# Output projection pairs: the residual sum is turned at once, without a provisional per-token factor

## The chip, the cores and the metric

The kernel runs on one core of a Trainium2 chip. Its five engines work beside each other, each through its own queue in order: TensorE (PE, matrix products; its weight loads are listed as PEld), VectorE (DVE), ScalarE (ACT), GpSimd (POOL) and SyncE (SP, which here only issues the DMA transfers). The metric is device time in microseconds (us), and the median of the runs counts.

## The reference

One decoder layer on 512 tokens of width 2048, all in float32. The middle is mixed by two kinds of heads, which are not touched here. What matters is the passage from the heads to the feed-forward part:

```python
mix = jnp.concatenate([out_a.astype(x.dtype), out_b.astype(x.dtype)], axis=-1)
x = x + mix @ w_out[l]
h2 = rms_norm(x, norm2_g[l])
x = x + (jax.nn.silu(h2 @ w_gate[l]) * (h2 @ w_up[l])) @ w_down[l]
```

`rms_norm` multiplies each token's row by one over the root of its mean square (plus 1e-6), and each column by `norm2_g`. The factor of a token is one number per row, so it can be applied behind a product with `w_gate` or `w_up` as well as ahead of it. `w_gate` and `w_up` have 5632 columns.

## The kernel before, in words

**Products.** Every large product is done two blocks of 512 columns at a time (a "pair", class `Pair`), by a scheme with seven half-size products, P1, P5, P6, P3, P7, P2, P4 in this order, of sums of quarters of the weights and of the activations. Each of the seven runs over the depth in 4 steps (3 in one operand of the last projection). I call one product at one step a group. A group is 12 matmuls on PE: 8 with the rounded ("high") part of the weights, tile `wh`, and 4 with the remainder, tile `wl`. ACT makes `wh` (L332), DVE makes `wl` (L336) and, in four products of seven, the difference of two weight quarters ahead of that (L257). There are two buffers of each, so ACT and DVE run at most about two groups ahead of PE. A pair of 4 steps has 28 groups. The two output projection pairs are called A and B here (groups A0 to A27, B0 to B27). Behind them come 11 feed-forward pairs for `w_gate` and `w_up` (the first one's groups are F0, F1, ...), and 6 pairs for `w_down`.

**Operands.** The activations stand in memory with the depth on the partitions. `Operand` splits each of the seven sums of a step into a high and a low part (`split`: a cast on ACT, L176, a subtraction on DVE, L177), all 128x512. The operand of the feed-forward pairs, `opn`, is read back from the DRAM tiles `xn_d0` to `xn_d7`, each with two halves of 256 tokens: `operand_jobs` builds its steps 0 and 1 from `xn_d0` to `xn_d3` in full, and `early_job` and `late_jobs` build steps 2 and 3 from `xn_d4` to `xn_d7`, the early ones through a tile `top`.

**Closing a product.** Four of the products (P3, P7, P2, P4) end an output block of 256 tokens by 512 columns. `final_out` then adds the residual (`residual`: two loads into tiles `q` and `k`, two sums on DVE, L1251, or L1248 for the block behind P4), stores the sum to `x1_d`, and squares it on ACT with a row sum into `ss2` (L1275). Eight such blocks, four in each pair, make the whole new x. Each is turned for the feed-forward part by `transposed_store`: 8 PE transposes (L1073), 4 ACT copies out of PSUM that multiply by `norm2_g` (L1084, into tiles `oT` and `PT`), two stores to `xn_d`. I call this a turn, and number the turns 1 to 8.

**The provisional factor.** Ahead of a turn, `scaled_store` multiplies the two tiles by `prox`, on ACT (L1259, into `qT` and `kT`). `prox` is one over the root of the mean square of each token's first 1024 columns, made on POOL by a power (L160, L161) once pair A has closed its last block. So in pair B each closed block is scaled and then turned one group later, while the four blocks of pair A wait until pair A is over: `first_columns` reloads them from `x1_d` (L1304, tiles `T` and `v`), scales and turns them during B's first groups. Then `operand_jobs` builds steps 0 and 1. `output_scales` makes the factor `rs2`, that corrects the provisional one, from all of `ss2`, in two sums on DVE and five small POOL instructions; the feed-forward pairs apply it where they close (L283, L299, L1346).

**What sets the order.** `stream` writes out the groups of all pairs in one sequence. In each group, between the high and the low matmuls, it calls a step function. That runs what is due in a list `deferred` (filled by `later(n, f)`: n steps from now), and then one step of the first generator in `background`. What a step issues lands in the engines' queues at that place; the framework may then move it by a few instructions.

## Time and profile before

| | |
|---|---|
| median of 3 runs | 1976.02 us (1974.23 to 1976.25) |
| profiled execution, its own time | 1977.08 us |
| its span, first to last instruction | 1975.2 us |
| PE busy | 1930.5 us, 98% |
| DVE busy | 1653.7 us, 84% |
| ACT busy | 1096.0 us, 55% |
| POOL busy | 55.0 us, 3% |
| granted TensorE clock, mean | 0.996 |
| last group of pair A to the end of turn 8 | about 642 to 748 us from the start |

The profile lists, for each instruction, its start, its duration, its engine and line, and in brackets how long the engine sat idle ahead of it and what ended that. A row may merge several instructions of one kind (x8). Durations of neighbours on one engine can overlap a little, so the time that an instruction takes in a full queue is read from start to start.

### The profile page before, as it was taken

The numbers are of one execution on the slowest core, as the hardware profiler recorded it, in microseconds if no ns is written. First come the engines' busy times: TensorE is split into PE (matmuls) and PEld (weight loads), VectorE is DVE, ScalarE is ACT, GpSimd is POOL, SyncE is SP. The second block draws the span as 40 slices with busy tenths as digits, with TensorE's granted clock in tenths as the row PEclk, the third lists the DMA queues.
The fourth block names the chain that finished last, engine by engine and source line by source line (L and its number), as shares of the span: only waits on it lengthen the run. The fifth ranks groups of instructions, "written<-read, shape, count | busy, mean of one in ns | idle before, by whom it ended". The sixth has DMA issues, their size and how long they took to land.

```text
span 1975.2 us, 25806 instructions
## 1 busy us (share of the span) xinstructions
PE 1930.5 (98%) x9226; PEld 1669.3 (85%) x9226; DVE 1653.7 (84%) x1850; ACT 1096.0 (55%) x1600; POOL 55.0 (3%) x81
## 2 busy tenths in 40 slices
PE   7999999999999989999999999999999999999998
PEld 6888888887878777888888888888888888888887
DVE  7997777768789789878878878878879989989977
ACT  7664564566676666545545545545446646546443
POOL 0000130011000001000000000000000000000000
PEclk9999999999999999999999999999999999999999
DMA  7347354444666584443543443543445855855662
GB/s 277 125 166 266 116 189 162 143 159 160 202 215 231 194 275 159 177 168 129 177 166 133 174 166 127 176 165 129 176 165 167 292 206 183 293 190 177 235 213 75
DMA packets 184505, 360.45 MB, mean 182 GB/s; under 512 B 16198, under 2 KB 94863, under 8 KB 184376
## 3 DMA queue, kind: packets, MB, share of 16 engines
q1 hardware_dynamic: 184168, 358.72, 52.8%
q8 instruction: 72, 1.18, 0.2%
q14 instruction: 57, 0.47, 0.1%
q10 hardware_dynamic: 208, 0.08, 0.0%
...
## 4 chain that ended last, share of the span: by engine, by line
PE 79%; DVE 8%; DMA 8%; issue 3%; ACT 1%; SPq 1%; POOL 0%; DVEq 0%; ACTq 0%; POOLq 0%
PE acc L362 70%; DVE wl L336 3%; PE acc L430 3%; DVE wa L257 2%; PE bank L1073 1%; PE bank L980 1%; DMA k<-y_d 1%; PE bank L958 1%; DVE AS L177 1%; DMA T<-p_d 1%; DMA xn_d<-oT 1%; DMA k<-in_gw 1%; DVE seed L1251 1%; PE bank L973 0%; PE bank L430 0%
## 5 line engine op out<-in xcount | busy, mean ns | idle before, releaser
L362 PE MATMUL acc<-wh,AS 128*128 128x512 f32 x3008 | 713.5, 380 | 1.5 <-DVE AS L177 1.0
L362 PEld LDWEIGHTS acc<-wh,AS 128*128 128x128 f32 x3008 | 567.7, 189 | 84.0 <-DVE AS L177 1.8
L332 ACT CAST wh<-wa 128x1024 fp32r<-128x1024 f32 x376 | 394.0, 1048 | 400.3 <-PE acc L362 364.9
L362 PE MATMUL acc<-wh,AA 128*128 128x512 f32 x2256 | 536.4, 380 | 6.0 <-ACT wh L332 6.0
L336 DVE TENSOR_TENSOR wl<-wa,wh 128x1024 fp32r<-128x1024 f32 x376 | 457.0, 1219 | 80.1 <-ACT wh L332 47.5
L362 PEld LDWEIGHTS acc<-wh,AA 128*128 128x128 f32 x2256 | 426.5, 189 | 68.6 <-ACT wh L332 8.4
L362 PE MATMUL acc<-wl,AS 128*128 128x512 f32 x1504 | 394.4, 384 | 7.2 <-DVE wl L336 7.1
L362 PEld LDWEIGHTS acc<-wl,AS 128*128 128x128 f32 x1504 | 279.3, 189 | 59.3 <-DVE wl L336 19.0
L362 PE MATMUL acc<-wl,AA 128*128 128x512 f32 x1128 | 296.7, 385 | 0.4 <-DVE wl L336 0.4
L362 PEld LDWEIGHTS acc<-wl,AA 128*128 128x128 f32 x1128 | 210.6, 190 | 32.3 <-DVE wl L336 2.7
L332 ACT CAST wh<-wb 128x1024 fp32r<-128x1024 f32 x94 | 98.5, 1048 | 118.0 <-PE acc L362 114.7
L332 ACT CAST wh<-wc 128x1024 fp32r<-128x1024 f32 x94 | 98.4, 1046 | 111.2 <-PE acc L362 105.4
L332 ACT CAST wh<-wd 128x1024 fp32r<-128x1024 f32 x94 | 98.6, 1049 | 104.7 <-PE acc L362 99.8
L336 DVE TENSOR_TENSOR wl<-wc,wh 128x1024 fp32r<-128x1024 f32 x94 | 114.8, 1221 | 41.2 <-ACT wh L332 40.9
L336 DVE TENSOR_TENSOR wl<-wd,wh 128x1024 fp32r<-128x1024 f32 x94 | 114.6, 1221 | 39.1 <-ACT wh L332 30.2
L257 DVE TENSOR_TENSOR wa<-wc,wa 128x1024 f32<-128x1024 f32 x94 | 114.6, 1222 | 35.7 <-DMA wc<-in_w_gate 20.0
L336 DVE TENSOR_TENSOR wl<-wb,wh 128x1024 fp32r<-128x1024 f32 x94 | 114.4, 1218 | 7.0 <-ACT wh L332 6.6
L257 DVE TENSOR_TENSOR wb<-wd,wb 128x1024 f32<-128x1024 f32 x94 | 114.5, 1218 | 0.4
L257 DVE TENSOR_TENSOR wa<-wb,wa 128x1024 f32<-128x1024 f32 x94 | 113.6, 1219 | 0.8
L257 DVE TENSOR_TENSOR wa<-wd,wa 128x1024 f32<-128x1024 f32 x94 | 113.0, 1217 | 0.2
L299 DVE SCALAR_TENSOR_TENSOR seed<-acc,rs,seed 128x512 f32<-128x512 f32 x96 | 70.6, 746 | 29.6 <-PE acc L362 29.6
L283 ACT ACTIVATE seed<-acc,rs 128x512 f32<-128x512 f32 x96 | 60.8, 683 | 3.1 <-DMA wc<-in_w_in 1.7
...
## 6 DMA issues: line engine op xcount, KB each, us to landing
...
```

The source lines that it names most:

```text
L177: nc.vector.tensor_tensor(a[:, :, 1, :], src, a[:, :, 0, :].bitcast(F32), op=ALU.subtract)
L257: nc.vector.tensor_tensor(src, self.quarter(one, g), src, op=ALU.subtract)
L283: nc.scalar.activation(halves(t), unfolded(src[m]), AF.Copy, scale=self.scale(half, m))
L299: nc.vector.scalar_tensor_tensor(halves(seed[m]), unfolded(src[m]), self.scale(half, m), halves(seed[m]), op0=ALU.mult, op1=ALU.add,)
L332: nc.scalar.copy(high[k], sources[k])
L336: nc.vector.tensor_tensor(low[k], sources.pop(k), high[k].bitcast(F32), op=ALU.subtract)
L362: nc.tensor.matmul(p.dst[prod][m], a[:, jj, hl, m * P : (m + 1) * P], folded(w[:, jj, :]), start=fresh and g == 0 and len(terms) == 2 and ...
L430: recent["pe"] = nc.tensor.matmul(dst[prod][m], a[:, jj, hl, m * P : (m + 1) * P], folded(w[:, jj, :]), start=fresh and g == 0 and len(ter ...
L958: nc.tensor.matmul(lp[:, :n], qh[:, b * P : (b + 1) * P], kh[:, :n], start=True, stop=True)
L980: nc.tensor.matmul(op, vh[:, k, :], lgs[b][:, k * P : (k + 1) * P], start=(k == 0), stop=(k == b))
L1073: nc.tensor.transpose(bk[:, jj, m * P : (m + 1) * P], tiles[m][:, f : f + P], ident)
L1251: nc.vector.tensor_tensor(tiles[m], tiles[m], r, op=ALU.add)
```

## The change

Nothing is multiplied by a provisional factor any more. In both pairs, `final_out` gives the summed tiles themselves to `transposed_store`, one step after the sum, so turns 1 to 3 move from pair B into pair A, and turn 4 to B's second group. With that go the 8 reloads from `x1_d`, the 16 scalings L1259 and `prox`. `operand_jobs` is put into the background at turn 4, at B's second step instead of its first, but without the eight steps of `first_columns` ahead of it. The factor `rs2` is now that of the whole row, made in three parts, one step apart, in the feed-forward groups F1 to F3: a sum and a scaling on DVE; a logarithm and an exponential on ACT; a correcting step of three small DVE instructions. All POOL work on factors of this norm goes.

```diff
-    part2 = const([P, 4], "part2")
-    prox = const([P, 4], "prox")
+    ms2 = const([P, 4], "ms2")
+    rt2 = const([P, 4], "rt2")
...
-    def scaled_store(tiles, rows, half, dsts, k0):
-        xs = []
-        for m in range(2):
-            s = work(("qT", "kT")[m])
-            nc.scalar.activation(s, tiles[m], AF.Copy, scale=prox[:, rows[m] : rows[m] + 1])
-            xs.append(s)
-        return lambda: transposed_store(xs, half, dsts, g2[:, k0 : k0 + 4])
...
-            if second:
-                turn = scaled_store(tiles, rows, tok, xn_d[2 * ch : 2 * ch + 2], 4 * ch)
-
-                def rest():
-                    turn()
-                    if which == 1 and half == 1:
-                        background.extend(early_job(opn, g, tops[g], False) for g in (2, 3))
-                        background.append(late_jobs(opn, ((2, 3),), tops, bots, False))
-
-                later(1, rest)
-                if which == 0 and half == 1:
-                    output_scales()
-            elif which == 0 and half == 1:
-                nc.vector.tensor_tensor(part2, ss2[:, :, 0], ss2[:, :, 1], op=ALU.add)
-                rsqrt_mean(prox, part2, D // 2)
-                background.append(first_columns())
-                background.append(operand_jobs(opn, tops, bots, 0, 2))
+            dsts, gains = xn_d[2 * ch : 2 * ch + 2], g2[:, 4 * ch : 4 * ch + 4]
+
+            def turn():
+                transposed_store(tiles, tok, dsts, gains)
+                if not second and which == 0 and half == 1:
+                    background.append(operand_jobs(opn, tops, bots, 0, 2))
+                elif second and which == 1 and half == 1:
+                    background.extend(early_job(opn, g, tops[g], False) for g in (2, 3))
+                    background.append(late_jobs(opn, ((2, 3),), tops, bots, False))
+
+            later(1, turn)
+            if second and which == 0 and half == 1:
+                for n in range(3):
+                    later(1 + n, lambda n=n: output_scales(n))
...
-    def first_columns():
-        for ch in range(2):
-            for tok in range(2):
-                tiles = []
-                for m in range(2):
-                    r = work(("T", "v")[m])
-                    load(r, x1_d[2 * tok + m][:, 512 * ch : 512 * ch + 512])
-                    tiles.append(r)
...
-    def output_scales():
-        tmp2 = const([P, 4], "tmp2")
-        nc.vector.tensor_tensor(tmp2, ss2[:, :, 2], ss2[:, :, 3], op=ALU.add)
-        nc.vector.tensor_tensor(tmp2, tmp2, part2, op=ALU.add)
-        rsqrt_mean(rs2, tmp2, D)
-        nc.gpsimd.tensor_scalar(part2, part2, 2.0 / D, EPS, op0=ALU.mult, op1=ALU.add)
-        nc.gpsimd.tensor_tensor(part2, part2, phalf, op=ALU.pow)
-        nc.gpsimd.tensor_tensor(rs2, rs2, part2, op=ALU.mult)
+    def output_scales(part):
+        if part == 0:
+            nc.vector.tensor_reduce(ms2, ss2, axis=mybir.AxisListType.X, op=ALU.add)
+            nc.vector.tensor_scalar(ms2, ms2, 1.0 / D, EPS, op0=ALU.mult, op1=ALU.add)
+        elif part == 1:
+            nc.scalar.activation(rt2, ms2, AF.Ln)
+            nc.scalar.activation(rt2, rt2, AF.Exp, scale=-0.5)
+        else:
+            nc.vector.scalar_tensor_tensor(ms2, ms2, -0.5, rt2, op0=ALU.mult, op1=ALU.mult)
+            nc.vector.tensor_tensor(ms2, ms2, rt2, op=ALU.mult)
+            nc.vector.scalar_tensor_tensor(rs2, ms2, 1.5, rt2, op0=ALU.add, op1=ALU.mult)
```

The rows below are instructions in the order of one engine's queue. They carry buffer numbers, and line numbers of the kernel they come from: after the change L332 is L330, L1084 is L1082, L1275 is L1265, L176 is L174, L1088 is L1086, L1127 is L1125.

ACT at the start of pair B, before. The casts L332 are those of groups B2, B3 and B4:

```order
L332 CAST wh_1163_6000<-wa_1153_5961 128x1024
L1275 ACTIVATE L_1158_5983,ss2_209<-k_1156_5976 128x512
L332 CAST wh_1170_6036<-wa_1164_6002 128x1024
L1259 ACTIVATE qT_1161_5992<-T_1159_5988,prox_211 128x512
L332 CAST wh_1177_6063<-wa_1145_5923 128x1024
L1259 ACTIVATE kT_1162_5994<-v_1160_5990,prox_211 128x512
L1084 ACTIVATE oT_1167_6019<-bank_1166_6014,g2_91 128x256 x2
L1084 ACTIVATE PT_1169_6028<-bank_1168_6023,g2_91 128x256 x2
```

ACT at the same place, after. The casts L330 are those of B2, B3 and B4 again; `r` are tiles read back from `xn_d` for the operand:

```order
L330 CAST wh_1171_6041<-wa_1165_6013 128x1024
L174 CAST AA11_1179_6075<-r_1178_6073 128x2x256
L1265 ACTIVATE L_1169_6032,ss2_207<-q_1167_6025 128x512
L1265 ACTIVATE L_1170_6035,ss2_207<-k_1168_6028 128x512
L330 CAST wh_1180_6082<-wa_1172_6043 128x1024
L1082 ACTIVATE oT_1175_6060<-bank_1174_6055,g2_89 128x256 x2
L1082 ACTIVATE PT_1177_6069<-bank_1176_6064,g2_89 128x256 x2
L174 CAST AA22_1184_6099<-r_1183_6097 128x2x256
L330 CAST wh_1185_6106<-wa_1153_5957 128x1024
```

The scaling of the reloaded tile is gone from between the casts of B3 and B4. In its place the operand's first two casts, of tiles read back from `xn_d`, stand ahead of the casts of B3 and B4, and the copies there are those of turn 4.

SP around the end of pair A, after: its stores of turn 3 and what is queued behind them (before, `xn_d0` is first stored after the reloads from `x1_d`):

```order
L1244 DMA q_1167_6025<-in_x 128x512
L1244 DMA k_1168_6028<-in_x 128x512
L221 DMA wd_1208_6210<-in_w_out 128x1024
L221 DMA wd_1212_6232<-in_w_out 128x1024
L1086 DMA xn_d0_199<-oT_1156_5974 256x1x256
L1086 DMA xn_d1_200<-PT_1158_5983 256x1x256
L221 DMA wd_1218_6258<-in_w_out 128x1024
L1125 DMA r_1183_6097<-xn_d0_199 128x2x256
L1125 DMA r_1188_6121<-xn_d2_201 128x2x256
L1263 DMA x1_d0_195<-q_1167_6025 128x512
```

The read-back into `r_1183`, which the cast AA22 above needs, now stands right behind the stores of turn 3 and ahead of the stores of A's last block.

DVE in the first groups of pair B, after (L334 makes `wl` of B2, B3, B4 and B5; L255 are weight differences; L175 and L191 belong to the operand):

```order
L334 TENSOR_TENSOR wl_1173_6045<-wa_1165_6013,wh_1171_6041 128x1024
L175 TENSOR_TENSOR AA11_1179_6075<-r_1178_6073,AA11_1179_6075 128x2x256
L255 TENSOR_TENSOR wa_1160_5993<-wb_1186_6108,wa_1160_5993 128x1024
L255 TENSOR_TENSOR wa_1165_6013<-wb_1193_6135,wa_1165_6013 128x1024
L334 TENSOR_TENSOR wl_1182_6087<-wa_1172_6043,wh_1180_6082 128x1024
L175 TENSOR_TENSOR AA22_1184_6099<-r_1183_6097,AA22_1184_6099 128x2x256
L255 TENSOR_TENSOR wa_1172_6043<-wb_1198_6161,wa_1172_6043 128x1024
L334 TENSOR_TENSOR wl_1187_6111<-wa_1153_5957,wh_1185_6106 128x1024
L191 TENSOR_TENSOR r_1183_6097<-r_1188_6121,r_1183_6097 128x512
L255 TENSOR_TENSOR wa_1153_5957<-wd_1204_6188,wa_1153_5957 128x1024
L175 TENSOR_TENSOR AS1_1189_6124<-r_1183_6097,AS1_1189_6124 128x2x256
L334 TENSOR_TENSOR wl_1194_6138<-wa_1160_5993,wh_1192_6133 128x1024
```

Before, DVE has no operand work until `wl` of B9 is made, and has made the weight differences of B4 to B11 and B16 to B19 ahead of that. Now the operand's work runs from B2 to B16, mixed with those differences: from behind `wl` of B0 to `wl` of B16 the queue holds 16 `wl`, 11 differences and 24 instructions of half that size.

8 lines of the change are left out of this document (removed).

## The prediction

> **What bounds the kernel now.** I read the page first, for the bound, then PE's waits between 640 and 760 us, the stretch that the change touches, and then PE's timeline of that stretch.
>
> ```profile
> span 1975.2 us, 25806 instructions
> PE 1930.5 (98%) x9226; PEld 1669.3 (85%) x9226; DVE 1653.7 (84%) x1850; ACT 1096.0 (55%) x1600; POOL 55.0 (3%) x81
> ```
>
> ```profile
> PE bank L1073 <- ACT qT L1259: 7.2, 3, 4.8
> PE acc L362 <- ACT wh L332: 3.5, 2, 2.5
> PE bank L1073 <- ACT kT L1259: 1.8, 2, 1.5
> ```
>
> PE is the bound, and the change takes no matmul or transpose away: all 64 transposes stay. So only time in which PE stands still, or runs at a lower clock, can move. In this stretch the scaling L1259 holds PE's transposes for 7.2 + 1.8 = 9.0 us, and late casts of `wh` hold its matmuls for 3.5 us.
>
> ```profile
> 644.65 1.89 PE L362 MATMUL acc<-wh,AA 128*128 128x512 f32 x8
> 647.24 1.89 PE L362 MATMUL acc<-wh,AA 128*128 128x512 f32 x8
> ...
> 649.85 1.67 PE L362 MATMUL acc<-wh,AA 128*128 128x512 f32 x7
> 656.28 0.69 PE L1073 MATMUL bank<-mats,qT 128*128 128x128 f32 x2 [4.76 <-ACT qT L1259]
> ...
> 663.78 0.38 PE L362 MATMUL acc<-wh,AS 128*128 128x512 f32 x1
> ...
> 703.68 1.89 PE L362 MATMUL acc<-wh,AS 128*128 128x512 f32 x8
> ...
> 729.08 1.89 PE L362 MATMUL acc<-wh,AA 128*128 128x512 f32 x8
> 735.81 1.99 PE L362 MATMUL acc<-wh,AA 128*128 128x512 f32 x8 [2.48 <-ACT wh L332]
> 750.50 1.89 PE L362 MATMUL acc<-wh,AA 128*128 128x512 f32 x8
> ...
> 811.93 1.89 PE L362 MATMUL acc<-wh,AA 128*128 128x512 f32 x8
> 815.40 1.89 PE L362 MATMUL acc<-wh,AA 128*128 128x512 f32 x8
> ```
>
> These are starts of groups. Undisturbed, a group takes 647.24 - 644.65 = 2.59 us; with a turn's 8 transposes in it 815.40 - 811.93 = 3.47, so a turn is 0.88. What a stretch takes beyond these is lost:
>
> - B2 to B4 (649.85 to 663.78, 2 groups, 1 turn): 13.93 - 5.18 - 0.88 = 7.87 us.
> - B4 to B18 (to 703.68, 14 groups, 3 turns): 39.90 - 36.26 - 2.64 = 1.0 us.
> - B18 to B26 (to 729.08, 8 groups, turns 5 and 6): 25.40 - 20.72 - 1.76 = 2.92 us.
> - B26 to F3 (to 750.50, 5 groups, turns 7 and 8): 21.42 - 12.95 - 1.76 = 6.71 us.
>
> Together 18.5 us, the most that could be won here.
>
> **The reload at the start of pair B (term 1).** The 7.87 us are the 4.76 of idling and a half clock behind it:
>
> ```profile
> 655.50 0.72 ACT L1259 ACTIVATE qT<-T,prox 128x512 f32<-128x512 f32 x1 [4.04 <-DMA T<-x_d]
> ```
>
> ```profile
> 651.50:656.30 4.80, 0.04 (x2) 0.02 (x1) 4.80 (x6) 0.72 (x1) 2.96 (x2) 0.91 0.50 138
> 656.30:662.00 5.70, 5.70 (x18) 4.78 (x19) 3.14 (x4) 2.18 (x4) 0.00 (x0) 0.50 0.49 178
> 730.00:740.00 10.00, 7.24 (x36) 5.75 (x35) 6.04 (x7) 5.91 (x12) 0.00 (x0) 1.00 0.87 273
> 750.00:760.00 10.00, 10.00 (x48) 8.55 (x46) 10.00 (x13) 7.48 (x11) 4.03 (x5) 1.00 0.62 205
> ```
>
> (After the length come the busy times of PE, PEld, DVE, ACT and POOL, then the clock.) The first tile comes back from DRAM late, ACT waits for it with B4's cast behind it, and PE with B2's last matmul behind its transposes. Then PE runs 5.7 us at clock 0.50, and loses about 2.9 by it; the 2.48 us gap at 735.81 left the clock at 1.00. The change removes the reload. What turn 4 waits for instead is the residual sum itself:
>
> ```profile
> 643.17 1.23 DVE L336 TENSOR_TENSOR wl<-wa,wh 128x1024 fp32r<-128x1024 f32 x1 [0.60 <-ACT wh L332]
> ...
> 649.07 0.69 DVE L1248 TENSOR_TENSOR k<-acc,k 128x512 f32<-128x512 f32 x1 [0.25 <-DMA k<-in_x]
> ```
>
> It ends at 649.76, and PE, by its groups above, would come to turn 4 (behind the high part of B1) at 647.24 + 1.73 = 648.97. But the three turns now in pair A bring PE there 2.64 us later: no wait. Between the ends 7.87 (nothing left) and 3.1 (a new wait as long as 4.76) I take 7.5 won.
>
> The Trainium skill (TensorE: Matmul & The Clock Gate, Part 1) says that an idle window of about 3.4 us halves PE's clock, and about 3.4 us of steady work restores it. Both gaps agree with it in kind. By its figure the half clock would cost an estimated 1.7 us here instead of 2.9, and my forecast would be some 1.2 us slower; the trace's 5.7 us at 0.50 decides.
>
> **The turns in pair A (term 2).** Three turns are moved work, 0 net. Turn 1 comes behind the high part of A18:
>
> ```profile
> 618.50 1.89 PE L362 MATMUL acc<-wh,AS 128*128 128x512 f32 x8
> 620.23 1.03 PE L362 MATMUL acc<-wl,AS 128*128 128x512 f32 x4
> ```
>
> ```profile
> 620.49 0.69 DVE L1251 TENSOR_TENSOR seed<-seed,k 128x512 f32<-128x512 f32 x1
> 621.09 0.69 DVE L177 TENSOR_TENSOR AA<-T,AA 128x512 fp32r<-128x512 f32 x1
> 621.69 1.22 DVE L336 TENSOR_TENSOR wl<-wb,wh 128x1024 fp32r<-128x1024 f32 x1
> 622.83 0.69 DVE L177 TENSOR_TENSOR AA<-qT,AA 128x512 fp32r<-128x512 f32 x1
> ```
>
> DVE's queue is the same up to there and full, and the second sum ends at 621.18, 0.95 us behind PE's arrival at 620.23. So PE waits 1.0 us, and the matmuls of A18 and A19 behind it. Turns 2 and 3 come later against their sums, but SP now issues the residual's loads behind the stores of the turn before: I add 0.3 and subtract 0.2 for small waits for `wl` that the delay covers. Cost 1.1, ends 0.3 and 4. The four ACT copies of a turn (oT, PT) come in A20 to A26, where ACT mostly waits for PE.
>
> **The operand's steps 0 and 1, earlier (term 3).** They now meet the weight differences on DVE. From start to start a full-size instruction takes 622.83 - 621.69 = 1.14 us, a half-size one 0.60. From `wl` of B0 to that of B16 the queue after the change holds 16 + 11 full and 24 half ones: 27 x 1.14 + 24 x 0.60 = 45.2 us. PE needs 16 x 2.59 + 0.88 = 42.3. Of the 2.9 excess, a head start covers 2.0: `wl` of B0 is ready at 644.40 (above), and PE uses it at 644.65 + 1.73 = 646.38. I take 1.5 lost, as casts in between wait on ACT, in place of the 1.0 lost now: cost 0.5, ends -1.0 and 3.
>
> **Turns 5 and 6 (term 4).** PE waits there for the scaling alone. Without it the tiles are ready one ACT instruction of 0.7 us and a queue place earlier. 0.5 is left of 2.92: 2.4 won, ends 0 and 2.92.
>
> **The stretch at the end of B (term 5).** Turns 7 and 8 lose the same wait (of the 7.2 us in three waits above, 4.76 are turn 4's place, and the other 2.4 those of turns 6 and 8): 1.2 won. The two waits for `wh`, 3.5 us, are behind ACT's cast of `top`, read back from `xn_d`:
>
> ```profile
> 734.19 0.62 ACT L176 CAST AA<-top 128x512 fp32r<-128x512 f32 x1 [2.77 <-DMA top<-xn_d]
> ```
>
> ```profile
> 723.26 0.56 SPq L1088 DMA_DIRECT2D xn_d<-oT  x1
> ```
>
> This chain starts at turn 6, which comes about 1 us earlier against its group: 1.0 won, 2.2 in all, ends -1 and 5.
>
> **The factor (term 6).** Five small DVE instructions replace two; the small POOL ones leave an idle engine.
>
> ```profile
> L642 DVE SCALAR_TENSOR_TENSOR rs<-nrs,rs x2: 161/161/161, 57.9 to 68.8; 128x2 f32<-128x2 f32 x2
> ```
>
> 3 x 0.16 = 0.5 us on a DVE that is busy 10.00 of 10.00 (the last window above). Cost 0.4, ends 0 and 0.6. The two on ACT (7.48 of 10 there) are free; if that cover went they would cost the same again. The first to need `rs2` is the scaling of F's first product, one step behind.
>
> **The sum.** -7.5 + 1.1 + 0.5 - 2.4 - 2.2 + 0.4 = -10.1 us. The profiled execution took 1977.08, of which 1975.2 are the span; it would become 1967.0. The median is 1.06 below it: 1976.02 - 10.1 = 1965.9, say 1966. All good ends give -7.87 + 0.3 - 1.0 - 2.92 - 5 = -16.5 (1959.5), all bad ones -3.1 + 4 + 3 + 0 + 1 + 0.6 = +5.5 (1981.5).
>
> **Rivals.** *The read-back takes the reload's place.* ACT's cast of B4 stands behind AA22, whose tile was stored at turn 3. From turn 3 (behind A26's high part) to B4 PE has 0.88 + 0.86 + 5 x 2.59 + 0.88 = 15.6 us. The chain: ACT's B0 cast and copies about 2.5, store and read-back, then AA22 0.6 and B4's cast 1.05. A round trip in pair B took 6.5 us:
>
> ```profile
> 677.06 0.56 SPq L1088 DMA_DIRECT2D xn_d<-oT  x1
> ```
>
> ```profile
> 683.60 0.69 DVE L193 TENSOR_TENSOR r<-r,r 128x512 f32<-128x512 f32 x1 [1.55 <-DMA r<-xn_d]
> ```
>
> That leaves 4.9 to spare; the one for `top`, 723.26 to 734.19, took 10.9 with DMA at 0.87 and would leave 0.5. If it is as late as today's reload, 7.87 come back: 1974, no measurable change. A chance of 0.11. The skill's rule would make any wait here under 3.4 us cost only itself; today's 2.48 us gap agrees.
>
> *DVE is the bound of pair B* (term 3 at its bad end and more, with small waits in each group): 5 us of the gain go, 1971. For it speaks the tally, against it that B17 to B27 are then empty. 0.12.
>
> *The other side: the residual's loads hold pair A.* SP now has the loads of `q` and `k` for turns 2 and 3 behind the stores of the turn before, and each store waits for ACT's copies. If they land over 4.8 us behind PE's arrival at both turns, PE idles as at 651, twice: 2 x 7.87 - 10.1 = +5.6, 1981.6. One such turn costs 7.9 and leaves a small gain; from both on it is slower. Against it: at turn 1's sums no load is waited for, and 0.25 us was the wait at 649.07. 0.07.
>
> **Chances and range.** The forecast (gain 6 to 15 us) 0.70. About 0.2% (4 us) is what a measurement of this kernel can tell from no change. Faster: 0.70 + 0.12 = 0.82; same 0.11; slower 0.07. The likeliest case gives 1961 to 1970; the range reaches to the first rival's 1974.
>
> **What would show it.** No L1259 and no PE gap over 1 us between B0 and B4, clock 1.00 there; a PE gap of about 1 us at turn 1 (A18); gaps for `wl` summing to some 1.5 us from B5 to B16; turns 5 to 8 each starting right behind their group; a gap for `wh` near the end of B that is still there, 1 us shorter. I am wrong if a gap of over 3 us shows anywhere from A18 to F3.

## The result, and the profile after

The changed kernel takes 1970.85 us (median of 12 runs, 1966.95 to 1975.06); the kernel before, run beside it on the same chip, takes 1975.18 (12 runs, 1972.88 to 1981.52). The ratio is 0.9977, with a 95% interval from 0.9968 to 0.9987: a gain of 4.5 us, between 2.6 and 6.3. The forecast was a gain of 10.1.

The page of the changed kernel, span and busy times:

```profile
span 1968.5 us, 25771 instructions
PE 1929.8 (98%) x9226; PEld 1669.3 (85%) x9226; DVE 1653.2 (84%) x1852; ACT 1086.9 (55%) x1586; POOL 47.4 (2%) x73
```

PE's waits in the same stretch as before (640 to 760 us), in all, times, longest:

```profile
PE acc L360 <- ACT wh L330: 4.3, 3, 2.7
PE bank L1071 <- DVE q L1246: 2.0, 1, 2.0
PE acc L360 <- DVE wl L334: 1.0, 2, 0.6
PE bank L1071 <- DVE k L1246: 0.6, 2, 0.3
```

The 9.0 us for the scaling are gone with it. The wait for `wh` has not shrunk (3.5 before, 4.3 now), and a wait of 2.0 for a residual sum is new. PE's timeline shows where these stand:

```profile
620.76 1.89 PE L360 MATMUL acc<-wh,AS 128*128 128x512 f32 x8
623.38 0.98 PE L1071 MATMUL bank<-mats,seed 128*128 128x128 f32 x7 [0.27 <-DVE seed L1249]
625.07 1.89 PE L360 MATMUL acc<-wh,AS 128*128 128x512 f32 x8
652.97 1.89 PE L360 MATMUL acc<-wh,AA 128*128 128x512 f32 x8
655.42 0.33 PE L1071 MATMUL bank<-mats,k 128*128 128x128 f32 x1 [0.33 <-DVE k L1246]
662.77 2.00 PE L360 MATMUL acc<-wh,AS 128*128 128x512 f32 x8 [0.32 <-ACT wh L330]
668.29 1.13 PE L360 MATMUL acc<-wl,AS 128*128 128x512 f32 x4 [0.62 <-DVE wl L334]
701.35 1.89 PE L360 MATMUL acc<-wh,AS 128*128 128x512 f32 x8
714.32 1.25 PE L1071 MATMUL bank<-mats,seed 128*128 128x128 f32 x8
724.04 1.89 PE L360 MATMUL acc<-wh,AA 128*128 128x512 f32 x8
730.40 1.99 PE L360 MATMUL acc<-wh,AA 128*128 128x512 f32 x8 [2.73 <-ACT wh L330]
737.05 1.99 PE L360 MATMUL acc<-wh,AA 128*128 128x512 f32 x8 [1.20 <-ACT wh L330]
741.05 0.33 PE L1071 MATMUL bank<-mats,q 128*128 128x128 f32 x1 [2.00 <-DVE q L1246]
747.60 1.67 PE L360 MATMUL acc<-wh,AA 128*128 128x512 f32 x7
792.25 1.89 PE L360 MATMUL acc<-wh,AA 128*128 128x512 f32 x8
```

These are A18 (620.76), A19 (625.07), B1 (652.97), B4 (662.77), B18 (701.35), B26 (724.04), F3 (747.60) and F20 (792.25), and between them the waits. The gap of 4.76 us at pair B's first turn (in B2) is now 0.33 (turn 4, in B1), turn 6 (714.32) starts without a wait, and the three long gaps left are B27's (730.40: 2.73), F1's (737.05: 1.20) and turn 8's (741.05: 2.00).

The same reckoning as in the prediction (start to start, less 2.59 us a group and 0.88 a turn) gives what each stretch loses. Both kernels were profiled a second time (e13 and e8 below), so each has two executions; the experiments have one each. Ratios are to the kernel before, run beside each.

| kernel | ratio (95%) | A18–B1 | B1–B4 | B4–B18 | B18–B26 | B26–F3 | F3–F20 |
|---|---|---|---|---|---|---|---|
| before, two executions | 1 | 0.25, 0.26 | 7.89, 7.52 | 1.00, 1.48 | 2.92, 2.91 | 6.71, 6.19 | 1.86, 3.08 |
| changed, two executions | 0.9977 (0.9968–0.9987), 0.9975 (0.9965–0.9985) | 1.08, 1.56 | 1.15, 0.62 | 2.32, 2.33 | 0.21, 0.21 | **8.85, 7.45** | 0.62, 1.72 |
| e1 one tile kept | 0.9972 (0.9962–0.9981) | 0.82 | 1.27 | 2.33 | 5.94 | 0.67 | 3.54 |
| e2 copy in pair B | 0.9975 (0.9964–0.9987) | 1.70 | 1.38 | 2.31 | 1.83 | 6.64 | 1.39 |
| e3 reload, no scaling | 1.0008 (0.9997–1.0018) | 0.20 | 8.47 | 2.10 | 2.11 | 6.45 | 0.98 |
| e4 turn 8 later | 0.9964 (0.9949–0.9978) | 1.53 | 0.39 | 2.32 | 0.21 | 7.07 | 2.76 |
| e5 both tiles kept | 0.9985 (0.9974–0.9995) | 1.59 | 1.78 | 2.33 | 0.21 | 8.28 | 3.97 |
| e7 stores on ACT's queue | 1.0004 (0.9993–1.0016) | 1.21 | 1.76 | 1.43 | 1.05 | 9.93 | 4.62 |
| e9 reads of `top` at once | 0.9961 (0.9947–0.9974) | 1.51 | 1.62 | 2.33 | 0.21 | 3.50 | 3.67 |
| e10 no residual load | 0.9941 (0.9925–0.9957) | 1.47 | 1.87 | 2.33 | 0.21 | 5.29 | 1.73 |
| e11 factor on POOL | 0.9979 (0.9970–0.9988) | 0.97 | 0.95 | 2.33 | 0.21 | 8.23 | 5.46 |
| e12 wider pacing | 0.9963 (0.9949–0.9976) | 1.52 | 0.00 | 1.87 | 0.78 | 4.91 | 2.42 |
| e14 e9 + e12 | 0.9952 (0.9941–0.9964) | 1.73 | 1.62 | 1.97 | 0.78 | 2.26 | 2.17 |
| e15 e14 + e4 | 0.9945 (0.9933–0.9957) | 1.15 | 0.50 | 1.97 | 0.78 | 0.88 | 3.32 |
| e16 e18 + e12 | 0.9930 (0.9918–0.9943) | 1.15 | 1.16 | 1.97 | 0.78 | 0.00 | 0.62 |
| e17 two constants back | 0.9961 (0.9946–0.9975) | 0.81 | 1.65 | 2.32 | 0.21 | 7.91 | 0.62 |
| e18 both kept, next reads later | 0.9929 (0.9916–0.9942) | 1.24 | 1.76 | 2.33 | 0.21 | 0.00 | 0.70 |

The sums for the two kernels: before 20.6 and 21.4 us, changed 14.2 and 13.9, so the stretch won 7.0 us on average. The start of pair B and turns 5 and 6 brought 9.5 of it, as the forecast had them (7.5 + 2.4). The end of pair B (B26 to F3), which was to bring 2.2, gave back 1.7. All the experiments on the cause go to that stretch; the others undo one part each.

One detail of its loss is not a wait. Windows of the changed kernel (length, then the busy times of PE, PEld, DVE, ACT and POOL, PE's clock, DMA's share and GB/s):

```profile
735.00:741.00 6.00, 2.85 (x12) 1.83 (x11) 4.78 (x7) 3.08 (x4) 0.00 (x0) 1.00 0.78 274
741.00:745.00 4.00, 3.68 (x14) 3.04 (x15) 4.00 (x7) 3.97 (x10) 0.00 (x0) 0.64 0.90 300
745.00:750.00 5.00, 5.00 (x24) 4.34 (x23) 4.53 (x9) 2.50 (x6) 0.00 (x0) 0.94 0.83 294
```

Behind the gap at turn 8 the clock falls to 0.64 and then 0.94: 4 x 0.36 + 5 x 0.06 = 1.7 us lost. So of the 8.85 us, 2.73 + 1.20 + 2.00 + 0.27 (the row behind 741.05) are waits and 1.7 is clock; the rest, 0.9, is spread around them.

### The profile page after: what moved, and what is told of

The parts are those of the page before. It is cut to its first block, busy times and chain, and to the rows that moved or that the text cites. A ratio compares the mean times of both kernels' runs of the same rounds, so it can differ in the third digit from the quotient of the medians.

```text
span 1968.5 us, 25771 instructions
## 1 busy us (share of the span) xinstructions
PE 1929.8 (98%) x9226; PEld 1669.3 (85%) x9226; DVE 1653.2 (84%) x1852; ACT 1086.9 (55%) x1586; POOL 47.4 (2%) x73
## 4 chain that ended last, share of the span: by engine, by line
PE 71%; DVE 7%; DMA 4%; issue 2%; ACT 1%; SPq 1%; POOL 0%; DVEq 0%; ACTq 0%; POOLq 0%
PE acc L360 67%; DVE wl L334 2%; PE bank L1071 1%; DVE wa L255 1%; PE bank L956 1%; DMA k<-y_d 1%; PE bank L978 1%; DMA xn_d<-oT 1%; DVE AS L175 1%; ACT wh L330 0%; PE bank L971 0%; DVE seed L1249 0%; DVE seed L293 0%; PE bank L947 0%; DMA r<-mix_d 0%
## 5 line engine op out<-in xcount | busy, mean ns | idle before, releaser
L330 ACT CAST wh<-wa 128x1024 fp32r<-128x1024 f32 x376 | 393.6, 1048 | 399.4 <-PE acc L360 367.6
L334 DVE TENSOR_TENSOR wl<-wa,wh 128x1024 fp32r<-128x1024 f32 x376 | 457.3, 1220 | 72.5 <-ACT wh L330 41.4
L330 ACT CAST wh<-wb 128x1024 fp32r<-128x1024 f32 x94 | 98.5, 1048 | 120.4 <-PE acc L360 111.2
L330 ACT CAST wh<-wc 128x1024 fp32r<-128x1024 f32 x94 | 98.4, 1047 | 112.6 <-PE acc L360 106.2
L330 ACT CAST wh<-wd 128x1024 fp32r<-128x1024 f32 x94 | 98.6, 1049 | 105.0 <-PE acc L360 99.9
L334 DVE TENSOR_TENSOR wl<-wc,wh 128x1024 fp32r<-128x1024 f32 x94 | 114.7, 1221 | 39.7 <-ACT wh L330 39.4
L334 DVE TENSOR_TENSOR wl<-wd,wh 128x1024 fp32r<-128x1024 f32 x94 | 114.6, 1221 | 39.5 <-ACT wh L330 30.2
L255 DVE TENSOR_TENSOR wa<-wc,wa 128x1024 f32<-128x1024 f32 x94 | 114.6, 1223 | 37.0 <-DMA wc<-in_w_gate 21.0
L334 DVE TENSOR_TENSOR wl<-wb,wh 128x1024 fp32r<-128x1024 f32 x94 | 114.3, 1219 | 6.7 <-ACT wh L330 6.3
L255 DVE TENSOR_TENSOR wb<-wd,wb 128x1024 f32<-128x1024 f32 x94 | 114.6, 1219 | 0.5
L255 DVE TENSOR_TENSOR wa<-wb,wa 128x1024 f32<-128x1024 f32 x94 | 113.7, 1220 | 0.8
L255 DVE TENSOR_TENSOR wa<-wd,wa 128x1024 f32<-128x1024 f32 x94 | 113.1, 1218 | 0.1
```

The lines of the kernel that those rows point to most:

```text
L255: nc.vector.tensor_tensor(src, self.quarter(one, g), src, op=ALU.subtract)
L330: nc.scalar.copy(high[k], sources[k])
L334: nc.vector.tensor_tensor(low[k], sources.pop(k), high[k].bitcast(F32), op=ALU.subtract)
```

## The experiments

**Which part of the change brought what**

*e3: the reload back, without the scaling.* Turns 1 to 4 stand in pair B again, on tiles read back from DRAM.

```diff
-            later(1, turn)
+            if second:
+                later(1, turn)
+            elif which == 0 and half == 1:
+                background.append(first_columns())
+                background.append(operand_jobs(opn, tops, bots, 0, 2))
...
+    def first_columns():
...
+                    load(r, x1_d[2 * tok + m][:, 512 * ch : 512 * ch + 512])
...
+                transposed_store(tiles, tok, xn_d[2 * ch : 2 * ch + 2], g2[:, 4 * ch : 4 * ch + 4])
```

> The changed kernel, but turns 1 to 4 stand in pair B again, each on tiles read back from DRAM, now without the scaling: this tells the reload from the scaling. Theory 1 (the reload was what PE waited for): a gap of 3 to 5 us stands at turn 4's old place behind B2 again, the clock halves behind it, B1 to B4 loses 6 to 8 us instead of 1.15, and pair A loses nothing: 1975 to 1978 us. Theory 2 (the scaling on ACT was): B1 to B4 loses at most 2 us, and the time is within 1.5 us of 1970.9.

The ratio is 1.0008: with the reload alone the whole gain is gone. PE's waits from 640 to 760 us now name the transfer itself:

```profile
PE bank L1071 <- DMA T<-x_d: 6.1, 2, 5.6
```

B1 to B4 loses 8.47 us (less two turns, which stand in B2 and B3), and A18 to B1 only 0.20. Theory 1 holds: it was the reload, not ACT's scaling, that PE stood for at the start of pair B, and its removal is what makes the changed kernel faster.

*e2: the copy on ACT back in pair B*, ahead of turns 5 to 8, with scale one.

```diff
+            if second:
+                xs = []
+                for m in range(2):
+                    s = work(("qT", "kT")[m])
+                    nc.scalar.activation(s, tiles[m], AF.Copy, scale=1.0)
+                    xs.append(s)
+                tiles = xs
```

> The changed kernel, but in pair B the summed tiles go through a copy on ACT (scale 1.0) ahead of turns 5 to 8, where the kernel before scaled them: the change's part in pair B undone, with the same results. Theory 1 (the copy on ACT was what PE waited for in turns 5 and 6): B18 to B26 loses 2.9 us again instead of 0.21, and B26 to F3 loses within 1 us of the 6.7 of the kernel before, since turns 7 and 8 then fall where they fell before; together 0.5 to 2.5 us slower than the changed kernel or as fast (1970.9 to 1973). Theory 2 (what was lost at the end of pair B has nothing to do with the turns' places): B26 to F3 loses 8 to 9.5 us as in the changed kernel, and the time is 2.5 to 4 us above it (1973.4 to 1975).

The ratio is 0.9975, that of the changed kernel: pair B's half of the change is worth nothing that these runs can show. B18 to B26 lost 1.83, less than the 2.9 expected, and B26 to F3 6.64; together 8.5, as much as the 9.1 and 7.7 of the changed kernel. That is theory 1's side: the end loses what it lost in the kernel before, and the time stays. What turns 5 and 6 win, the end of B loses again. One row of PE and one of ACT show the form it takes here:

```profile
734.11 0.43 PE L1071 MATMUL bank<-mats,kT 128*128 128x128 f32 x1 [4.38 <-ACT kT L1274]
```

```profile
732.90 0.62 ACT L174 CAST AA<-top 128x512 fp32r<-128x512 f32 x1 [5.08 <-DMA top<-xn_d]
```

The copy `kT` stands on ACT behind the cast of `top`, which waits for the read-back.

*e11: the factor made on POOL again*, in one go.

```diff
-                for n in range(3):
-                    later(1 + n, lambda n=n: output_scales(n))
+                nc.vector.tensor_reduce(ms2, ss2, axis=mybir.AxisListType.X, op=ALU.add)
+                rsqrt_mean(rs2, ms2, D)
```

> The changed kernel, but the norm's factor is made as before, by POOL's power function, in one go behind one small sum on DVE: the factor's part of the change undone. Theory 1 (five small instructions on DVE cost next to nothing): within 0.7 us of the changed kernel, F3 to F20 losing 0.6 to 1.9 us as before. Theory 4 (the factor on DVE and ACT delays the differences of weights in F): 1 to 2 us less than the changed kernel.

0.9979 against 0.9977 and 0.9975: no difference in time that these runs can show, as theory 1 has it. Its one profiled execution lost 5.46 us from F3 to F20, outside the 0.6 to 1.9 expected: one small POOL instruction stood for 11 us there, ACT waited for it, and behind that the clock was 0.57 from 760 to 764 us (1.7 us lost). With one execution it is open whether this is usual.

```profile
745.55 10.99 POOL L158 TENSOR_SCALAR rs<-ms 128x4 f32<-128x4 f32 x1 [274.67 <-DVE ms L1280]
```

```profile
757.66 1.26 ACT L281 ACTIVATE seed<-acc,rs 128x512 f32<-128x512 f32 x2 [5.13 <-POOL rs L159]
```

*e12: steps 0 and 1 of the operand in pair B at two of three groups.*

```diff
-    pair(..., final_out(1), paced([1] * 28))
+    pair(..., final_out(1), paced([0, 1, 1, 0, 1, 1, ..., 0, 1, 1, 1]))
```

> The changed kernel, but the operand's steps 0 and 1 in pair B are taken at two of three groups instead of at each, so that they meet the differences of weights on DVE less densely; the reads of `top` come as late as before. Theory 3 (the loss from B4 to B18, 2.32 us here against 1.00 in the kernel before, comes from that meeting): B4 to B18 loses 0.5 to 1.5 us, and the time is 0.8 to 1.8 us less than the changed kernel's. Against it: B4 to B18 stays at 2.0 to 2.6 us, and the time within 0.7 us.

The time fell by somewhat more than theory 3 expected (0.9963, 0.0013 or 2.6 us below the changed kernel's, where the intervals overlap), but not where it said: B4 to B18 still loses 1.87. The rest shows at B1 to B4 (nothing lost) and at B26 to F3 (4.91). The two waits for `wl` from B4 to B18 (0.62 and 0.37 us) are gone, but six groups there are each some 0.3 us longer instead. So the thinner meeting on DVE wins some 0.4 us from B4 to B18, and what the rest of that loss comes from is open.

**Where the gain at the end of pair B went**

The chain there begins with turn 6. In the changed kernel the rows of SP's queue and of ACT are:

```profile
717.34 0.94 SPq L221 DMA_DIRECT2D wb<-in_w_up  x2
718.37 0.90 SPq L1086 DMA_DIRECT2D xn_d<-oT  x1
...
725.59 0.57 SPq L1125 DMA_DIRECT2D top<-xn_d  x1
```

```profile
728.79 0.62 ACT L174 CAST AA<-top 128x512 fp32r<-128x512 f32 x1 [4.94 <-DMA top<-xn_d]
735.44 0.62 ACT L174 CAST AA<-top 128x512 fp32r<-128x512 f32 x1 [2.15 <-DMA top<-xn_d]
```

Turn 6 starts at 714.32; its store goes out 4.05 us later, behind two loads of weights; 7.2 us after that SP issues the read, since it waits for the store to land and holds all behind it; 3.2 us later ACT's cast can begin. Together 14.5 us; the kernel before took 720.20 to 734.19, 14.0. Before:

```profile
720.20 0.44 PE L1073 MATMUL bank<-mats,qT 128*128 128x128 f32 x2 [0.79 <-ACT qT L1259]
```

B27, whose `wh` stands on ACT behind that cast, is due 13.2 us behind turn 6 here (724.04 + 2.59 + 0.88 = 727.51) and 12.4 before (729.08 + 3.47 = 732.55). So turn 6 does come 0.8 us earlier against its consumer, but the chain behind it is 0.5 longer; B27 starts 2.89 us late instead of 3.26. In the second executions the chain takes 14.7 us (e8) and 13.3 (e13), and B27 is late by 3.15 and 2.55: on average nothing is won.

*e1: turn 6's tile kept in SBUF* and cast from there; turn 5's half still comes back from DRAM.

```diff
+                last = second and which == 1 and half == 1
+                kept = apool.tile([P, 2, 2, 256], F32, name=nm("kept"), tag="A") if last else None
-                transposed_store(tiles, tok, dsts, gains)
+                transposed_store(tiles, tok, dsts, gains, spare=kept)
...
-                    background.extend(early_job(opn, g, tops[g], False) for g in (2, 3))
+                    background.append(early_direct(kept))
```

> The changed kernel, but the tile that turn 6 makes is kept in SBUF and cast from there into the operand's steps 2 and 3, so that this part does not come back from DRAM; its store stays. Theory 1 (the cast of `top` waits for the way through DRAM, and that way was not made shorter): both waits of PE for `wh` near the end of pair B (2.73 and 1.20 us in the changed kernel) go, the clock stays at 1.00 there, and the stretch from B26 to F3 loses 2 to 5 us instead of 8.85; the kernel takes 1964 to 1967 us, 4 to 7 us less than the changed one. Theory 2 (ACT has too much work there, and the cast would be late anyway): the waits for `wh` stay within 0.5 us of 2.73 and 1.20, and the time within 1 us of 1970.9.

Neither theory: both waits for `wh` went and B26 to F3 lost 0.67, but the time moved by less than its uncertainty (0.9972), since a new wait of 4.57 us stands two groups earlier. The subtraction on DVE waits for the half that is still read, and `wl` of B25 stands behind it:

```profile
724.83 1.37 DVE L1294 TENSOR_TENSOR top<-kept,top 128x512 f32<-128x512 f32 x2 [6.43 <-DMA top<-xn_d]
```

*e5: both tiles kept*, the order of the work as the kernel makes it.

```diff
+                if second and which == 1:
+                    kept[half] = apool.tile([P, 2, 2, 256], F32, name=nm("kept"), tag="A")
-                transposed_store(tiles, tok, dsts, gains)
+                transposed_store(tiles, tok, dsts, gains, spare=kept.get(half) if which else None)
...
-                    background.extend(early_job(opn, g, tops[g], False) for g in (2, 3))
+                    background.append(early_direct(kept[1], kept[0]))
```

> As e1, but the tiles of both turns 5 and 6 are kept in SBUF, so that no part of the operand's steps 2 and 3 made there is read back from DRAM. Theory 1 (in every kernel so far PE's largest wait near the end of B goes back to one read-back of `top`, in e1 the 4.57 us for `wl` behind the subtraction of the half that was still read): no PE wait over 1 us from B18 to F3, the clock at 1.00, B18 to F3 together loses 1 to 3 us instead of 9.06, and the kernel takes 5 to 8 us less than the changed one. Theory 2 (the wait moves on to the next thing that is late, the other reads or the DVE work behind): the loss from B18 to F20 stays within 2 us of 9.7, and the time within 2 us of the changed kernel's.

2 us above the changed kernel (0.9985 against 0.9975 on the same chip; the intervals overlap), where theory 1 expected 5 to 8 less; theory 2's mechanism is what the rows show. The operand's later steps now come sooner, and their reads take the place of the ones left out: on SP's queue they wait for turn 6's store, with the weights for F1 behind them.

```profile
723.45 0.60 SPq L221 DMA_DIRECT2D wb<-in_w_up  x1
729.18 0.57 SPq L1159 DMA_DIRECT2D qT<-xn_d  x1
729.87 0.57 SPq L1159 DMA_DIRECT2D kT<-xn_d  x1
730.53 0.55 SPq L221 DMA_DIRECT2D wd<-in_w_up  x1
```

```profile
738.32 1.23 DVE L255 TENSOR_TENSOR wb<-wd,wb 128x1024 f32<-128x1024 f32 x1 [4.65 <-DMA wd<-in_w_up]
```

SP issues nothing from 724.05 to 729.18, the weights land late, DVE waits 4.65 us for them, and PE 4.21 at turn 8.

*e4: turn 8 one step later.*

```diff
-            later(1, turn)
+            later(2 if second and which == 0 and half == 1 else 1, turn)
```

> The changed kernel, but turn 8 is put one step later, behind one more group. Theory 1 (turn 8 now comes on PE ahead of F1's low part while the sum of q stands on DVE behind F1's wl, so that PE waits 2.00 + 0.27 us, and with two other gaps close to it the clock drops to 0.64): this wait goes and the clock stays at 1.00 from 741 to 747 us; B26 to F3 loses 4.5 to 6.5 us instead of 8.85, and the time is 1966.5 to 1968.5 us. Theory 2 (DVE is late there whatever PE does, and the wait would only move to the next wl or wh): B26 to F4 loses within 1 us of the changed kernel's, and the time is within 1 us of 1970.9.

The wait at turn 8 went, but B27's wait for `wh` was 3.11 us here and the clock behind it fell (0.66 from 730 to 740), so B26 to F3 lost 7.07 and not the 4.5 to 6.5 of theory 1. The median is 0.0012 below the changed kernel's, within both intervals: turn 8's place is a minor part.

*e7: the turns' stores issued on ACT's queue.*

```diff
-            store(dsts[b][:, :, half * 256 : (half + 1) * 256], d)
+            (nc.scalar.dma_start if gains is not None else store)(
+                dsts[b][:, :, half * 256 : (half + 1) * 256], d
+            )
```

> The changed kernel, but the stores of the turns are issued on ACT's queue right behind the copies, no longer on SP's queue behind loads of weights and of the residual. Theory 1b (the order on SP's queue makes the way of `top` long): the store of turn 6 is issued some 1.5 us earlier against its turn, the cast of `top` comes 1 to 3 us earlier against turn 6, and the time is 1 to 4 us less than the changed kernel's. Theory 1a (full DMA engines): the cast comes within 0.7 us of 14.5 us behind the start of turn 6, and the time within 1.5 us of the changed kernel's.

Both theories missed: the gain is gone (1.0004). From turn 6 to the cast it took 714.56 to 731.40, 16.8 us, more than before, with the read still issued 10.7 us behind the turn. Moving the store to another queue does not shorten the way, and DMA is at 1.04 from 720 to 730.

*e10: no residual loads in pair B.*

```diff
-            load(r, src(rows[m], c0))
+            s = r
+            if c0 < 1024:
+                load(r, src(rows[m], c0))
+            else:
+                s = mats.rearrange("p a b -> p (a b)")
```

> The changed kernel, but pair B adds constants that stay in SBUF in place of the input's columns: eight loads of 256 KB, 2.1 of the 14.7 MB moved from 700 to 750 us, are left out (so the sum lacks the input there); DVE does the same work. Theory 1a (the way of `top` through DRAM is as long as it is because the DMA engines are full, 0.97 from 720 to 730): from turn 6 to the cast of `top` at least 1.5 us less than 14.5, the waits for `wh` (2.73 + 1.20 us) below 2 together, 2 to 5 us less than the changed kernel. Theory 1b (two transfers one behind the other and their place on SP's queue): the waits stay within 1 us of 3.9, and the time within 1.5 us.

(A first form, e6, with a tile of zeros of its own has no time: the tile leaves 21.28 KB a partition of SBUF for a pool that needs 22.75. e10 adds a constant that is there anyway.)

With fewer bytes the way from turn 6 to the cast is 715.66 to 728.43, 12.8 us, 1.7 less, and the ratio 0.9941, some 7 us better than the changed kernel's (0.9977, 0.9975), though its stages lose only 1 us less in the one profiled execution (12.9 against 14.2 and 13.9); where the other 6 come from is open. The waits for `wh` are gone, but one of 2.17 us for `wl` stands in their place. Theory 1a holds so far as that bytes in the queue lengthen the chain; of the 1.7 us, 1.4 are those between turn 6 and its store (2.66 instead of 4.05), which is a place on SP's queue as much as a full engine. From the store to the read it is 6.9 us against 7.2.

*e9: the same reads and bytes, the reads issued at once.* The casts and subtractions of `top` were written among F0 to F3.

```diff
-                    background.extend(early_job(opn, g, tops[g], False) for g in (2, 3))
+                    background.append(early_late())
...
+            for h in range(2):
+                part(tops[g], h)(held[g][:, h])
+        yield
+        while not begun:
+            yield
+        for g in (2, 3):
+            opn.split("A11", g, held[g][:, 0])
+            yield
+        for g in (2, 3):
+            r21 = held[g][:, 1]
+            nc.vector.tensor_tensor(r21, held[g][:, 0], r21, op=ALU.subtract)
+            opn.split("S3", g, r21)
+            yield
...
-            finish(lambda: ("S3", 3) in opn.t)
+            begun.append(1)
```

> The changed kernel, but all four reads of `top` are issued at once behind turn 6, and the casts and subtractions on them stand one to four groups later, among the groups F0 to F3, so that no cast or difference of weights stands on ACT's or DVE's queue behind data that are still under way; the bytes moved are the same. Theory 1c (PE loses at the end of B because instructions that are ready stand in order behind those that wait for the reads): the waits for `wh` at F0 and F2 (2.73 + 1.20 us) and what they do to the clock go, B26 to F3 loses 2 to 5 us instead of 8.85, and the time is 3 to 6 us less than the changed kernel's. Theory 1a (the DMA engines are full in that stretch, whatever stands where): other data are late in their place, and the time is within 1.5 us of the changed kernel's.

(The gaps that this text puts at F0 and F2 are those of B27 and F1.) The edit did less than it says. The framework moved the casts forward again: on ACT the first still stands ahead of the `wh` of B27, and waits as before.

```profile
730.56 0.62 ACT L174 CAST AA<-top 128x512 fp32r<-128x512 f32 x1 [4.68 <-DMA top<-xn_d]
731.08 1.04 ACT L330 CAST wh<-wa 128x1024 fp32r<-128x1024 f32 x1
732.03 0.61 ACT L174 CAST AA<-top 128x512 fp32r<-128x512 f32 x1
```

What is new is that the reads for both steps go out together (at 727.18; in the changed kernel the second step's went out 3.8 us behind the first's). So theory 1c was not tried by it. The second step's casts find their data: F1's wait for `wh` is gone, turn 8's is 0.50, the clock stays at 1.00, and B26 to F3 loses 3.50, of which 2.03 are B27's wait. The ratio is 0.9961; F3 to F20 lost 3.67 against 0.62 and 1.72, so part of the lateness only moved on.

*e14 and e15: e9 with e12, and with e4 as well.* The edits are those.

> The changed kernel with the late casts of e9 and the operand's steps 0 and 1 of pair B at two of three groups as in e12. If the two act in different places (e9 from B26 on, e12 from B1 to B18), their gains add: A18 to F20 takes 167.5 to 169 us (171.3 in the changed kernel, 170.1 and 168.8 in e9 and e12), and the ratio to the kernel before is 0.995 within 0.001. If both gain the same microseconds (a read of `top` that comes earlier against its group), it is 0.9955 to 0.9965, as each alone.

> As e14, with turn 8 one step later as in e4. If the wait at turn 8 (0.50 us in e9, 2.00 in the changed kernel) is only what the late reads leave on DVE's queue, it is already gone and this run is within 1 us of e14; if it is turn 8's place, 1 to 2 us less than e14.

e14 is at 0.9952 and A18 to F20 takes 167.8 us (743.83 at F3, 790.03 at F20): the gains add. e15 is at 0.9945, 1.4 us better than e14 with overlapping intervals, and its stretch 165.9; what is left is 3.3 us behind F3.

*e16 and e18: both tiles kept, and the reads that follow later.* The steps on the kept tiles are drawn out to F0 and behind, so that the operand's later steps, and their reads, begin later than in e5. e16 has e12's pacing too, e18 not. The edit is e5's, with

```diff
+    def early_kept(top, other):
+        for g in (2, 3):
+            opn.split("A11", g, top[:, g - 2])
+            yield
+        while not begun:
+            yield
+        for g in (2, 3):
+            r = other[:, g - 2]
+            nc.vector.tensor_tensor(r, top[:, g - 2], r, op=ALU.subtract)
+            opn.split("S3", g, r)
+            yield
...
-            finish(lambda: ("S3", 3) in opn.t)
+            begun.append(1)
...
+    paces = {0: [0, 1, 1, 0, 1, 1, 1, 1, 1, 1] + [0] * 5, 10: [0] * 6}
```

> As e14, but the tiles of turns 5 and 6 are kept in SBUF as in e5, so nothing of the operand's steps 2 and 3 that is needed from F0 to F7 comes back from DRAM; the later steps' reads stand where they stand in the changed kernel, not earlier as they did in e5. Theory 1b (the way through DRAM, 7.2 us from the issue of the store to that of the read, is what PE waits for): no wait of PE over 1 us from B18 to F3, B18 to F3 loses under 3 us, and the time is 1 to 4 us less than e14. Theory 1a (full DMA engines make whatever comes by DMA late): a wait of 2 to 5 us for weights or for the input's columns behind turn 7 or 8, as in e5, and the time is that of e14 or more.

> As e16, but with the operand's steps 0 and 1 at each group again: the tiles of turns 5 and 6 kept in SBUF and the order behind F0 alone. If these two are what clears the end of pair B, B18 to F3 loses under 2 us here too, and the ratio to the kernel before is 0.993 to 0.9945 (e16 has 0.9930, the wider pacing being worth 0.5 to 2 us); if it was the wider pacing that made room, a wait of over 1.5 us stands between B26 and F3 again and the ratio is 0.995 or more.

0.9930 and 0.9929: a gain of 14 us on the kernel before (1962.75 and 1964.10 us). From B26 to F3 nothing is lost at all. Three of the four casts run right behind turn 6's copies (in e18 from 720.39 on), and none waits for a transfer. All that PE waits for in e16 from 640 to 760 us:

```profile
PE bank L1071 <- DVE k L1246: 0.3, 1, 0.3
PE acc L360 <- ACT wh L330: 0.3, 1, 0.3
PE bank L1071 <- DVE seed L1249: 0.3, 1, 0.3
```

and two of its windows:

```profile
725.00:735.00 10.00, 10.00 (x56) 8.88 (x55) 9.57 (x12) 7.41 (x13) 0.00 (x0) 1.00 1.01 343
735.00:745.00 10.00, 10.00 (x48) 8.77 (x47) 9.99 (x15) 7.31 (x14) 0.00 (x0) 1.00 0.70 228
```

DMA's share is 1.01 in the first, and PE is busy all the time. So full DMA engines are not by themselves what PE loses by (theory 1a falls as the main cause); what it lost by is the way of `top` through DRAM, and what stood in order behind it. e5 against e18 shows that keeping the tiles is not enough: in e18 the weights `wd` go out at 726.52, 9.4 us behind turn 6, in e5 12.8 us behind it. The wider pacing is not needed (e18 against e16).

**What the medians show less of than the stages**

*e8 and e13: both kernels once more.*

> The changed kernel once more, on the chip of e5 to e7, as their yardstick. If the loss at the end of pair B belongs to the kernel and not to one execution, B26 to F3 loses 7 to 10 us again, with waits of PE for `wh` and for the sum of q; if it was chance, it loses under 6. The ratio to the kernel before should be 0.9977 within 0.001.

> The kernel before once more with a profile of its own, since all that is said of its stages rests on one execution. If that execution was a usual one, B1 to B4 loses 7 to 9 us again, B18 to B26 2 to 4, B26 to F3 5.5 to 8, and A18 to F20 takes 176.5 to 179 us (177.89 in the first; 171.49 and 171.15 in the two of the changed kernel). If it was chance, A18 to F20 takes under 176, and the gain in the traces is nearer to the 4.6 us of the medians than to the 6.6 of the stages.

The stages came out alike (table), and e13's median is that of the kernel before, 1.0001 (0.9992 to 1.0010). So the stage gain of 7.0 us is no chance of one execution, and the medians (4.5 and 4.9 us) show some 2 us less. Part of that lies ahead of A18: the 40 groups that end two groups ahead of it take 144.04 and 144.10 us in the kernel before and 145.31 and 145.52 in the changed one, with the same instructions in the same order on every engine up to there, but for one at the very start, on POOL, that sets a constant the change drops. The four profiled spans agree with the medians rather than with the stretch: 1968.5 and 1971.2 us against 1975.2 and 1972.8, 4.2 less on average. Of the 2.8 us that the stretch gained beyond that, 1.0 are lost ahead of these 40 groups, 1.3 in them and 0.4 behind F20, where two executions of one kernel differ by 3.4 and 2.6 us.

*e17: two small constants back.*

```diff
+    phalf = const([P, 4], "phalf")
+    nc.gpsimd.memset(phalf, 0.5)
...
+    tmp2 = const([P, 4], "tmp2")
+    nc.gpsimd.memset(tmp2, 0.5)
```

> The changed kernel with two small constants of four columns again that it had dropped (one set at the start of the program, as before), so that everything in SBUF lies where it lay in the kernel before. In the traces the changed kernels reach A18 some 3 us later than the kernel before (616 against 613 us at its side of pair A's block), though the instructions up to there stand in the same order. If the place in SBUF or that first instruction on POOL does it, groups 140 to 180 of the program take 144.0 to 144.3 us again, and the time falls by 1 to 3 us against the changed kernel; if it is chance or something else, they take 144.6 to 147.4 as in the other changed kernels, and the time stays within 1 us of it.

Those 40 groups took 143.99 us, as in the kernel before, and the ratio is 0.9961 (0.9946 to 0.9975), 0.0014 to 0.0016 below the changed kernel's. (The 616 and 613 us of this text are the start of the group two ahead of A18.) It points to where the data lie in SBUF, or to that first POOL instruction. But it is one profiled execution, and the intervals overlap. And the 144.6 to 147.4 us of the other kernels hold a half clock: in 7 of the 16 executions without the two constants the clock is 0.50 for 3.4 us between 474 and 480 us, which costs 1.7 us, in none of the three with them. Without that cost two of the seven come to 143.6 (e11) and 144.2 us (e15). So the 40 groups do not tell the constants apart from chance: not settled.

## Why the prediction was right and wrong

The sign and the main mechanism were right, and 1970.85 us lies in the range that reaches to 1974; the gain of 4.5 us lies below the 6 to 15 of the forecast. By its terms (measured: mean of two executions each):

- **The reload (term 1).** 7.5 predicted, 6.8 measured from B1 to B4 (7.71 to 0.89). Right, with e3 as the proof. In one of the two executions the sums of turn 4 are late by 0.33 us, where I had no wait.
- **Turns in pair A (term 2).** Cost 1.1 predicted, 1.06 measured (0.26 to 1.32). Turn 1 is as forecast: from A18 to A19 it is 625.07 - 620.76 = 4.31 us, 0.84 more than 3.47 (1.00 in e8). The row's gap of 0.27 is only a part of that, since the first transposes too stand until their sums are made.
- **Steps 0 and 1 (term 3).** Cost 0.5 predicted, 1.1 measured (1.24 to 2.33), and only 0.4 of the loss goes with a wider pacing. The tally of DVE's work gave the sign; the size was short.
- **Turns 5 and 6 (term 4).** 2.4 predicted, 2.7 measured at its place. e2 shows that it is worth nothing to the time as long as the end of B stands as it does.
- **The end of B (term 5): the step that failed.** "This chain starts at turn 6, which comes about 1 us earlier against its group: 1.0 won", and 1.2 at turns 7 and 8. Measured: 1.7 us more lost (6.45 to 8.15). Turn 6 did come 0.8 us earlier, but the term took the chain behind it as unchanged, and that grew from 14.0 and 13.3 us to 14.5 and 14.7: the store of turn 6 waited behind loads of weights (4.05 and 4.12 us behind the turn against 3.06 and 3.13). So from B26 to F1 nothing was won (4.6 and 4.3 us lost before, 4.4 and 4.7 after). The 1.7 stand from F1 to F3 (2.1 and 1.9 before, 4.5 and 2.7 after), where turn 8's wait, 1.66 and 1.49 before, became 2.27 in both executions (2.00 and 0.27): no longer for ACT's copy but for the sum of q, on a DVE that the late `top` holds up. I had priced each wait by the engine that the row named, and not by what that engine was itself waiting for.
- **The factor (term 6).** Cost 0.4 predicted, none seen: F3 to F20 lost 1.3 us less (2.47 to 1.17), where two executions of one kernel differ by 1.1 and 1.2, and e11 shows no difference in time.

For term 5, turn 8 before, and DVE ahead of its sum, before and after:

```profile
746.40 0.44 PE L1073 MATMUL bank<-mats,qT 128*128 128x128 f32 x2 [1.66 <-ACT qT L1259]
```

```profile
738.78 1.23 DVE L257 TENSOR_TENSOR wa<-wb,wa 128x1024 f32<-128x1024 f32 x1
741.35 0.69 DVE L177 TENSOR_TENSOR AA<-top,AA 128x512 fp32r<-128x512 f32 x1 [1.34 <-ACT AA L176]
```

```profile
736.22 0.69 DVE L214 TENSOR_TENSOR top<-top 128x512 f32<-128x512 f32 x1 [2.88 <-DMA top<-xn_d]
737.43 1.22 DVE L255 TENSOR_TENSOR wa<-wb,wa 128x1024 f32<-128x1024 f32 x1
740.31 0.68 DVE L1246 TENSOR_TENSOR q<-acc,q 128x512 f32<-128x512 f32 x1
```

In both executions of the kernel before, a difference of weights stands ahead of DVE's wait for `top`, in both of the changed kernel behind it. From the end of that wait to the sum of q it is 4.09 us after (736.22 to 740.31) and 2.95 before (741.35 to 744.30); the 1.14 between them are that difference. This is read from the rows; no run moves it alone. That the late `top` is behind the wait, runs do show: it is 0.77 in e9, whose second step finds its data, and no wait is left there in e16 and e18.

With the measured terms the sum is -6.8 + 1.1 + 1.1 - 2.7 + 1.7 - 1.3 = -6.9 in place of -10.1; the medians' 4.5 lack another 2.4. That is the second thing that the sum had wrong: it put everything ahead of A18 and behind F20 at nothing. The profiled spans show the loss there (2.8 us), most of it ahead of A18; its cause stays open.

Of the rivals, "DVE is the bound of pair B" gave the time that came (1971), but not for its reason: e12 thins DVE's work from B4 to B18 and wins little there, so that the time agreed was luck. The read-back did not take the reload's place at B4 (0.32 us); it was late at the other end. Of the signs named, turn 1 cost what was forecast, the gaps for `wl` came to 1.0 and not 1.5, turns 5 to 7 started right behind their groups and turn 8 did not, the gap for `wh` was there but longer (2.73 against 2.48), and none was over 3 us.

On the clock, the rule weighed in the prediction (the Trainium skill, TensorE: Matmul & The Clock Gate, Part 1) names an idle window of about 3.4 us ahead of a drop. Here gaps of 2.39 us (e13) and 2.99 (e8) at B27 were enough, where 2.48 in the first execution was not, so the length of a gap alone does not decide, and the prediction's sentence that a wait under 3.4 us costs only itself did not hold. What the Trainium skill says there of the recovery agrees with the windows: in the changed kernel the 1.7 us that it lost are 3.4 us at half clock.

The rows of e13 and e8, to be read against the 1.89 to 1.99 us that the same eight matmuls take at full clock:

```profile
734.65 3.02 PE L362 MATMUL acc<-wh,AA 128*128 128x512 f32 x8 [2.39 <-ACT wh L332]
```

```profile
730.27 3.44 PE L360 MATMUL acc<-wh,AA 128*128 128x512 f32 x8 [2.99 <-ACT wh L330]
```

Shorter gaps show it more plainly. In all 19 executions PE waits 1.43 to 1.93 us for a transfer between 471 and 477 us. In seven the clock is halved behind that (gaps of 1.65 to 1.92), in twelve it is not (1.43 to 1.93). The changed kernel and e15 with the same gap, 1.81 us:

```profile
474.00:481.00 7.00, 5.73 (x36) 4.90 (x37) 6.98 (x13) 4.40 (x9) 0.00 (x0) 1.00 0.60 195
474.00:481.00 7.00, 6.22 (x31) 5.63 (x32) 5.98 (x12) 3.67 (x8) 0.00 (x0) 0.76 0.49 154
```
